# Modulation loads under the feed-forward products, moved to another queue and to half of the steps, and two copies moved between engines

## The chip, the cores and the metric

The kernel runs on one core of a Trainium2 chip. The metric is the device time of one execution in microseconds; a kernel's time is the median of several executions. The engines of the core work side by side: TensorE (PE, with its weight loads shown apart as PEld), VectorE (DVE), ScalarE (ACT), GpSimd (POOL) and SyncE (SP). SP here does nothing but start transfers between the main memory and the on-chip memory; GpSimd starts some too. An engine's instructions run in the order of its queue.

## What is computed

One layer of a hybrid encoder block on 512 tokens of width 2048, in 32-bit floats, and a final norm. The reference, cut to what matters here:

```python
c_act = jax.nn.silu(c)                       # c: one row of 2048
mod = c_act @ w_ada[l] + b_ada[l]            # 2048 x 12288: six rows of 2048
sh1, sc1, g1, sh2, sc2, g2 = split(mod, 6)
h = rms_norm(x, norm1_w[l]) * (1.0 + sc1) + sh1
qa, ka, va, qb, kb, vb, ga, gb = split(h @ w_in[l])
ya = global_gqa(...); yb = neighbourhood_attention(...)
merged = sigmoid(ga) * (ya @ w_oa[l]) + sigmoid(gb) * (yb @ w_ob[l])
x = x + g1 * (merged @ w_out[l])
h2 = rms_norm(x, norm2_w[l]) * (1.0 + sc2) + sh2
ff = (silu(h2 @ w_ffn_gate[l]) * (h2 @ w_ffn_up[l])) @ w_ffn_down[l]
x = x + g2 * ff
return rms_norm(x, final_w)
```

`g2` is needed only where `ff` is added, at the very end. It is one row times a 2048 x 2048 part of `w_ada`, which is 16 MB to be read.

## The kernel before

**Products.** Each float is split into a high part in the type that TensorE multiplies (fp32r) and a low part that holds the rest, and a product is three: high by high, high by low, low by high (`mm3`, lines 141 to 143). `split` (lines 132 to 134) makes the parts: the high one by a copy on ScalarE, the low one by a subtraction on VectorE. Weights come from main memory as raw tiles of 512 KB (`raw`, loaded by SP on line 148) and are split into `whl`. There are five buffers of each kind from the output projection on: four and three in one pool, one and two in a pool `wq` that takes every fifth raw tile (`buffer`, lines 106 to 111).

**The feed-forward products.** Gate and up projections are computed in groups of 512 columns, eleven for the gate and eleven for the up weights; the first gate group is done in another way, so 21 groups remain (`group7`, line 873, called on line 981). A group multiplies by a scheme with seven block products in place of eight. It has four steps of a quarter of the depth each. A step loads two raw tiles, forms sums of their blocks (`ta`, `tb`, lines 838 to 841), splits them, and runs 84 matmuls. At the end of a group the seven sums are taken out of their banks and combined (lines 892 to 899); the next group's products go to the same banks, so its third product waits for line 896.

**The modulation under them.** The row `g2` is formed in four pieces of 512 (`ada_gate`, line 312), called gates below. For each, eight raw tiles of `w_ada` (two parts of 128 x 512 each) are loaded by SP (line 273), and each part is multiplied by its column of `c_act` and added to `acc` by VectorE (line 288): 16 sums per gate. GpSimd clears `acc` first (line 281), and SP puts the bias row into it (line 282). Then TensorE adds up over the 128 partitions (line 320, `total`), VectorE copies one row (line 322) and SP stores it (line 323). This is a background job: a generator in the list `bg`, of which `pump` (line 166) runs one piece per call. `group7` calls `pump` at its second, third and fourth step (line 878), after the step's weights and before its matmuls, so a raw tile of `w_ada` is loaded and used in the same call. `total` is set down in the list `soon` with a count and runs some calls later; with one buffer for `acc`, the generator then waits out three calls before the next gate begins. A gate takes 11 calls.

**The order.** The order of each engine's queue is fixed before the run by the framework, by program order as a priority, by when it expects operands and buffers to be there. It may draw an instruction forward past earlier ones of its engine: a sum of line 288 often stands among the weights of an earlier step. The raw tiles of the first pool go to whichever buffer is free; the one in `wq` is fixed.

**The merge.** Lines 707 to 714 compute `merged` in pairs of feature tiles, `j` in steps of two, and split each into `mx[j // 2]` (named `m0h`, `m0l` to `m7h`, `m7l`). Each pair takes two units of `w_oa` and two of `w_ob`. The output projection (`w_out_pass`, line 750) starts right behind the last pair and begins with the first feature tiles.

The lines the change touches:

Of the kernel before, what the change touches and what calls it, by code (L numbers as in the profile page):

```python
# [19 lines left out]
P = 128  # L20
D = 2048
T = 512
NT = T // P
KT = D // P
# [63 lines left out]
def encoder_block(ctx: ExitStack, tc, xp, xT, c, w_ada, ada1_w, b_ada, norm1_w, w_in, q_norm_w, k_norm_w, tb,  # L88
                  w_oa, w_ob, w_out, norm2_w, w_gate, w_up, w_down, final_w, rope, wmask, out):
    nc = tc.nc  # L90
    V, S, G = nc.vector, nc.scalar, nc.gpsimd
# [21 lines left out]
    def raw_tile(name="raw"):  # L113
        return buffer("raw", [P, 1024], F32, wbufs["raw"], name)
# [7 lines left out]
    def bank(tag):  # L122
        return ps.tile([P, 512], F32, tag=tag, name=tag, bufs={"mm": 4, "S": 2, "T": 1, "Y": 1}[tag])
# [8 lines left out]
    def split(hi, lo, src, eng=V):  # L132
        S.activation(hi, src, AF.Copy)  # L133
        eng.tensor_sub(lo, src, hi)  # L134
# [5 lines left out]
    def mm3(o, lh, ll, rh, rl, start, stop, **kw):  # L140
        nc.tensor.matmul(o, lh, rh, start=start, stop=False, **kw)  # L141
        nc.tensor.matmul(o, lh, rl, start=False, stop=False, **kw)  # L142
        nc.tensor.matmul(o, ll, rh, start=False, stop=stop, **kw)  # L143

    def unit(w, k0, nk, c0, ncol):
        raw = raw_tile()
        r3 = raw[:, :nk * ncol].rearrange("p (k n) -> p k n", k=nk)
        nc.sync.dma_start(r3, w[k0 * P:(k0 + nk) * P, c0:c0 + ncol].rearrange("(k p) n -> p k n", p=P))
        return raw[:, :nk * ncol], r3
# [8 lines left out]
    bg = []  # L158
# [3 lines left out]
    soon = []  # L162
# [3 lines left out]
    def pump():  # L166
        due = [f for n, f in soon if n <= 0]
        soon[:] = [(n - 1, f) for n, f in soon if n > 0]
        for f in due:
            f()  # L170
        if later:
            later.pop(0)()
        for _ in range(pace["steps"]):
            advance()

    def advance():
        if bg:
            try:
                next(bg[0])
            except StopIteration:  # L180
                bg.pop(0)
                advance()

    def form1(ws, c0, g, xs, banks, evac, eng=V):

        nk = 8 // g
        n = len(xs)
        for k0 in range(0, n, nk):
            m = min(nk, n - k0)
            for w, bs in zip(ws, banks):  # L190
                hi, lo = wsplit(w, k0, m, c0, g * P, eng)
                for kk in range(m):
                    xh, xl = xs[k0 + kk]
                    for j in range(g):
                        sl = slice(j * P, (j + 1) * P)
                        mm3(bs[j], hi[:, kk, sl], lo[:, kk, sl], xh, xl, k0 + kk == 0, k0 + kk == n - 1)
                pump()
        for wi, bs in enumerate(banks):
            for j in range(g):
                evac(wi, j, bs[j])  # L200
# [58 lines left out]
    t2 = const.tile([P, KT], F32, name="t2")  # L259

    accp = aside
    ada_room = {"bank": "Y", "bufs": 2}

    def ada_units(cols, w):

        nj = len(cols)
        nk = 1024 // (nj * w)
        for k0 in range(0, KT, nk):
            raw = raw_tile()
            r4 = raw.rearrange("p (k c n) -> p k c n", k=nk, c=nj)  # L270
            for j, col in enumerate(cols):
                src = w_ada[k0 * P:(k0 + nk) * P, col:col + w]
                nc.sync.dma_start(r4[:, :, j], src.rearrange("(k p) n -> p k n", p=P))
            yield [(k0 + e, raw[:, e * nj * w:(e + 1) * nj * w]) for e in range(nk)]

    def ada_acc(cols, w, bias):


        acc = accp.tile([P, 512], F32, tag="acc", name="acc", bufs=ada_room["bufs"])[:, :len(cols) * w]
        if bias:  # L280
            G.memset(acc, 0.0)
            nc.sync.dma_start(acc[0:1, :], b_ada[:, cols[0]:cols[0] + w])
        for parts in ada_units(cols, w):
            for k, part in parts:
                if k == 0 and not bias:
                    V.tensor_scalar(acc, part, cact[:, k:k + 1], None, op0=ALU.mult)
                else:
                    V.scalar_tensor_tensor(acc, part, cact[:, k:k + 1], acc, op0=ALU.mult, op1=ALU.add)  # L288
            yield None
        yield acc  # L290
# [21 lines left out]
    def ada_gate(col, q, dst):  # L312

        for acc in ada_acc((col + q * 512,), 512, True):
            if acc is None:
                yield

        def total():
            y = bank(ada_room["bank"])
            nc.tensor.matmul(y, ones, acc, start=True, stop=True)  # L320
            o = io.tile([P, 512], F32, tag="io", name="ada_o")
            V.tensor_copy(o[0:1, :], y[0:1, :])
            nc.sync.dma_start(dst[q], o[0:1, :])

        soon.append((1, total))
        if ada_room["bufs"] == 1:
            yield
            yield
            yield

    def rows(dst, src):
# [261 lines left out]
    bg.extend(ada_mod(3 * D, 4 * D, k, 2, (s2, b_sc2, n2, t2, b_sh2)) for k in range(0, KT, 2))  # L593
    g1_d, g2_d = ([dram.tile([1, 512], F32, name=f"g{n}d{q}") for q in range(4)] for n in (1, 2))
    bg.extend(ada_gate(2 * D, q, g1_d) for q in range(4))
    pace["steps"] = 2
    gates(sg_b, GB, 0, 8)
# [78 lines left out]
    def half(t, n=2):  # L676
        return t.rearrange("p (a q n) -> p a q n", q=2, n=256) if n == 2 else t.rearrange("p (q n) -> p q n", q=2)
# [15 lines left out]
    mT = [tuple(Tokens(half(t)[:, :, k % 2]) for t in mx[k // 2]) for k in range(KT)]  # L693

    def gated(src, dst):
        def evac(w, j, b):
            g = io.tile([P, T], F32, tag="io", name="g")
            nc.sync.dma_start(g, src[j])
            if any(src[j] is t for t in sg_a[:12]):
                S.activation(g, g, AF.Sigmoid)  # L700
            o = p_y.tile([P, T], F32, tag="o", name="o", bufs=4)
            V.tensor_mul(o, g, b)
            dst.append(o)
        return evac

    turn = itertools.cycle(("mm", "mm", "S"))
    for j in range(0, KT, 2):
        ma, mb = [], []
        for w, ys, sg, to in ((w_oa, yT[:8], sg_a, ma), (w_ob, yT[8:], sg_b, mb)):
            tag = next(turn)  # L710
            form1([w], j * P, 2, ys, [[bank(tag), bank(tag)]], gated(sg[j:], to))
        for e in range(2):
            V.tensor_add(ma[e], ma[e], mb[e])
            split(*(t.t for t in mT[j + e]), ma[e].rearrange("p (t n) -> p t n", t=2))
    p_y.release()
    aside.release()
    wq = tc.alloc_tile_pool(name="wq", bufs=1, side="right", reuse_waits="tile")
# [86 lines left out]
    norm((2, 3))  # L804
    gpool.release()
    accp = tc.alloc_tile_pool(name="accp", bufs=1, side="left", reuse_waits="tile")
    ada_room.update(bank="T", bufs=1)

# [62 lines left out]
    def group7(wsrc, xs, order, dst):  # L873

        bk = {r: bank(BANK[r]) for r in ORDER}
        for n, s in enumerate(order):
            w = wsrc(s)
            if n:
                pump()
            for r in ORDER:  # L880
                (wh, wl), (xh, xl) = w[r], xs[s][r]
                for q in range(2):
                    for c in range(2):
                        o = bk[r][:, c * 256:(c + 1) * 256]
                        cs = slice(c * P, (c + 1) * P)
                        first, last = n == 0 and q == 0 and c == 0, n == len(order) - 1 and q == 1
                        mm3(o, wh[:, q, cs], wl[:, q, cs], xh[:, q], xl[:, q], first, last, skip_group_check=True)
        p = {r: b.rearrange("p (c n) -> p c n", c=2) for r, b in bk.items()}
        (d11, d12), (d21, d22) = dst
        with tc.high_priority():  # L890
            p1 = io.tile([P, 512], F32, tag="io", name="p1").rearrange("p (c n) -> p c n", c=2)
            S.activation(p1, p[1], AF.Copy)
            V.tensor_add(d11, p[2], p1)
            V.tensor_add(d21, p[6], p1)
            V.tensor_add(d12, p[5], d21)
            V.tensor_add(d12, p[3], d12)  # L896
            V.tensor_add(d21, p[7], d21)
            V.tensor_add(d22, p[5], d21)  # L898
            V.tensor_sub(d21, d21, p[4])
# [9 lines left out]
    parts = [(s, a) for s in (2, 3, 0, 1) for a in range(2)]  # L909
# [54 lines left out]
    for n in range(FU):  # L964
        cs = []
        for w in (w_gate, w_up):
# [8 lines left out]
            def wsrc(s):  # L975
                d = wforms(w, 4 * s, n * 512)
                if s == 1 and n == FU - 1 and w is w_up:
                    first_pairs()
                return d
# [6 lines left out]
            V.tensor_mul(cs[1][:, sl], cs[1][:, sl], cs[0][:, sl])  # L986
        (nc.sync if n < FU - 1 else nc.gpsimd).dma_start(ff_d[n], cs[1])

    wbufs["at"] = 0
    for p in (c_p, f_x[1], f_x[0], ca, f_x[3], f_x[2], accp, p_m):  # L990
        p.release()
# [122 lines left out]
    ahead = {}  # L1114
# [70 lines left out]
    for cc in range(2, 4):  # L1185
        wt = p_s.tile([P, 4096 + 64], F32R, tag=f"a{3 - cc}", name=f"w{cc}")
        hi, lo = (wt[:, 48 + e * 2048:48 + (e + 1) * 2048] for e in range(2))
        for k in range(0, 4, 2):
            raw, _ = unit(w_down, f0 + k, 2, cc * 512, 512)
# [55 lines left out]
```

## Time and profile before

| what | value |
|---|---|
| time, median of 3 runs | 2639.69 us (2639.11 to 2649.6) |
| profiled execution | 2644.09 us, its span 2642.3 us |
| granted TensorE clock, mean | 0.992 |
| TensorE busy | 2569.5 us, 97% |
| VectorE busy | 1913.7 us, 72% |
| ScalarE busy | 1029.5 us, 39% |
| GpSimd busy | 95.1 us, 4% |
| groups of seven products end | 21 times, from about 1351 to 2150 us |
| last modulation sum | 1864.6 us |

How to read the profile: a row of a group of instructions gives line, engine, operation, the tile written and those read, how often, and durations in ns (least, median, most). A row of waits gives the engine and line that waited, what ended the wait, and total, number and longest in us. A row of the order of time gives start and duration in us, and in brackets how long the engine was idle before and what ended that. A row of a stretch gives its bounds and length, the busy time of PE, PEld, DVE, ACT and POOL with the number of instructions, the granted clock, and the DMA engines' share and rate. A busy TensorE isn't necessarily at its quickest, since its matmuls overlap.

### The profile page before, as it was taken

The numbers are of one execution on the slowest core, as the hardware profiler recorded it, in microseconds if no ns is written. First come the engines' busy times: TensorE is split into PE (matmuls) and PEld (weight loads), VectorE is DVE, ScalarE is ACT, GpSimd is POOL, SyncE is SP. The second block draws the span as 40 slices with busy tenths as digits, with TensorE's granted clock in tenths as the row PEclk, the third lists the DMA queues.
The fourth block names the chain that finished last, engine by engine and source line by source line (L and its number), as shares of the span: only waits on it lengthen the run. The fifth ranks groups of instructions, "written<-read, shape, count | busy, mean of one in ns | idle before, by whom it ended". The sixth has DMA issues, their size and how long they took to land. (4 is left out here: it accounts for less than half of the span.)

```text
span 2642.3 us, 40965 instructions
## 1 busy us (share of the span) xinstructions
PE 2569.5 (97%) x16569; PEld 2320.3 (88%) x16569; DVE 1913.7 (72%) x2708; ACT 1029.5 (39%) x1406; POOL 95.1 (4%) x134
## 2 busy tenths in 40 slices
PE   6999999999999999999999999999999999999998
PEld 5788878888788888788999999999999997999997
DVE  7985787766746544336798888888888885678767
ACT  5223544223333332226644433444444454334233
POOL 0100000001010000011000000000000000000000
PEclk8999999999999999999999999999999999999999
DMA  8864245974735844546454444545434456447463
GB/s 315 303 242 146 64 152 171 302 231 148 227 106 167 264 156 144 182 130 218 120 182 136 139 152 136 161 127 160 129 124 124 130 171 223 163 144 246 149 254 109
DMA packets 251949, 458.77 MB, mean 174 GB/s; under 512 B 16112, under 2 KB 102496, under 8 KB 243312
## 3 DMA queue, kind: packets, MB, share of 16 engines
q1 hardware_dynamic: 238208, 381.64, 45.3%
q0 software_dynamic: 12064, 71.31, 7.6%
q10 hardware_dynamic: 1488, 3.20, 0.3%
q8 instruction: 130, 2.13, 0.3%
q14 instruction: 59, 0.48, 0.1%
HBM read 412.03 MB, written 44.06 MB: 173 GB/s over the span
## 5 line engine op out<-in xcount | busy, mean ns | idle before, releaser
L133 ACT ACTIVATE whl<-raw 128x1024 fp32r<-128x1024 f32 (+1 forms) x483 | 463.6, 962 | 862.7 <-PE mm L143 274.4
L134 DVE TENSOR_TENSOR whl<-raw,whl 128x1024 fp32r<-128x1024 f32 (+1 forms) x483 | 533.2, 1113 | 309.9 <-ACT whl L133 301.5
L288 DVE SCALAR_TENSOR_TENSOR acc<-raw,cact,acc 128x512 f32<-128x512 f32 x248 | 187.3, 755 | 43.6 <-DMA raw<-in_w_ada 37.5
L133 ACT ACTIVATE whl<-tb 128x1024 fp32r<-128x1024 f32 x104 | 110.5, 1063 | 175.0 <-PE S L143 137.8
L133 ACT ACTIVATE whl<-ta 128x1024 fp32r<-128x1024 f32 x104 | 110.3, 1061 | 173.2 <-PE mm L143 123.8
L134 DVE TENSOR_TENSOR whl<-ta,whl 128x1024 fp32r<-128x1024 f32 x104 | 127.2, 1223 | 46.0 <-ACT whl L133 45.5
L134 DVE TENSOR_TENSOR whl<-tb,whl 128x1024 fp32r<-128x1024 f32 x104 | 127.0, 1221 | 15.6 <-ACT whl L133 14.5
L141 PE MATMUL mm<-x3h,whl 128*128 128x256 f32 x336 | 94.8, 282 | 13.6 <-DVE c L896 13.6
L838 DVE TENSOR_TENSOR ta<-raw 128x512 f32<-128x512 f32 x104 | 71.8, 690 | 49.1 <-DMA raw<-in_w_down 35.1
L141 PE MATMUL mm<-whl,a 128*128 128x256 f32 (+1 forms) x304 | 97.9, 322 | 3.5 <-ACT acc L1105 3.5
L839 DVE TENSOR_TENSOR ta<-raw,ta 128x512 f32<-128x512 f32 x104 | 71.7, 690 | 39.9 <-DMA raw<-in_w_down 22.2
L142 PE MATMUL mm<-whl,a 128*128 128x256 f32 (+1 forms) x304 | 97.8, 322 | 0.2 <-DVE whl L134 0.2
L143 PE MATMUL mm<-whl,a 128*128 128x256 f32 (+1 forms) x304 | 97.7, 321 | 0.0
L141 PE MATMUL mm<-x56h,whl 128*128 128x256 f32 x336 | 94.4, 281 | 1.3 <-DVE c L898 0.7
L142 PE MATMUL mm<-x3l,whl 128*128 128x256 f32 x336 | 94.2, 280 | 0.0
L143 PE MATMUL mm<-x3h,whl 128*128 128x256 f32 x336 | 94.1, 280 | 0.0
L142 PE MATMUL mm<-x56l,whl 128*128 128x256 f32 x336 | 93.8, 279 | 0.0
L143 PE MATMUL mm<-x56h,whl 128*128 128x256 f32 x336 | 93.7, 279 | 0.0
L143 PE MATMUL S<-x56h,whl 128*128 128x256 f32 x336 | 93.6, 279 | 0.0
L142 PE MATMUL S<-x56l,whl 128*128 128x256 f32 x336 | 93.6, 279 | 0.0
L141 PE MATMUL S<-x56h,whl 128*128 128x256 f32 x336 | 93.6, 279 | 0.0
L142 PE MATMUL mm<-whl,s 128*128 128x256 f32 x320 | 90.6, 283 | 2.2 <-DVE whl L134 2.2
(1479 smaller groups left out, 8508.7 us busy)
## 6 DMA issues: line engine op xcount, KB each, us to landing
raw<-in_w_in SPq DMA_DIRECT2D x133, 512.0 KB
raw<-in_w_gate SPq DMA_DIRECT2D x92, 512.0 KB
raw<-in_w_up SPq DMA_DIRECT2D x88, 512.0 KB
raw<-in_w_down SPq DMA_DIRECT2D x88, 512.0 KB
raw<-in_w_ada SPq DMA_DIRECT2D x128, 256.0 KB
raw<-in_w_ada SPq DMA_DIRECT2D x64, 512.0 KB
raw<-in_ada_w POOLq DMA_DIRECT2D x29, 1024.0 KB, 6.7
raw<-in_w_out SPq DMA_DIRECT2D x48, 512.0 KB
```

What stands on the lines that cost most here:

```text
L133: S.activation(hi, src, AF.Copy)
L134: eng.tensor_sub(lo, src, hi)
L141: nc.tensor.matmul(o, lh, rh, start=start, stop=False, **kw)
L142: nc.tensor.matmul(o, lh, rl, start=False, stop=False, **kw)
L143: nc.tensor.matmul(o, ll, rh, start=False, stop=stop, **kw)
L288: V.scalar_tensor_tensor(acc, part, cact[:, k:k + 1], acc, op0=ALU.mult, op1=ALU.add)
L838: V.tensor_sub(t1, b12, b11)
L839: V.tensor_sub(t2_, b22, t1)
```

## The change

The generator of the loads can run one load ahead: it keeps a list `ready`, and a call first issues the next load and then hands out the one before. Under the feed-forward products (`ahead=1`) the first call of a gate only loads, and the sums of a tile come one call after its load. The loads there are issued on GpSimd's queue. `group7` calls `pump` at its third and fourth step only. `total` is set down with count 0 in place of 1 and the generator waits out one call in place of three, so a gate takes 10 calls. After the groups a loop runs whatever is left. Before the feed-forward products (`ahead` 0, SP's queue, two buffers for `acc`) the job is as it was.

Apart from this, the high parts of the last two merged tiles (`j` = 14) are copied by VectorE instead of ScalarE.

```diff
-    ada_room = {"bank": "Y", "bufs": 2}
+    ada_room = {"bank": "Y", "bufs": 2, "ahead": 0, "queue": nc.sync}
...
-        for k0 in range(0, KT, nk):
+        def load(k0):
             raw = raw_tile()
             r4 = raw.rearrange("p (k c n) -> p k c n", k=nk, c=nj)
             for j, col in enumerate(cols):
                 src = w_ada[k0 * P:(k0 + nk) * P, col:col + w]
-                nc.sync.dma_start(r4[:, :, j], src.rearrange("(k p) n -> p k n", p=P))
-            yield [(k0 + e, raw[:, e * nj * w:(e + 1) * nj * w]) for e in range(nk)]
+                ada_room["queue"].dma_start(r4[:, :, j], src.rearrange("(k p) n -> p k n", p=P))
+            return [(k0 + e, raw[:, e * nj * w:(e + 1) * nj * w]) for e in range(nk)]
+
+        ready = []
+        for k0 in range(0, KT, nk):
+            ready.append(load(k0))
+            yield ready.pop(0) if len(ready) > ada_room["ahead"] else None
+        yield from ready
...
         for parts in ada_units(cols, w):
+            if parts is None:
+                yield None
+                continue
...
-        soon.append((1, total))
+        soon.append((ada_room["bufs"] - 1, total))
         if ada_room["bufs"] == 1:
-            yield
-            yield
             yield
...
-            split(*(t.t for t in mT[j + e]), ma[e].rearrange("p (t n) -> p t n", t=2))
+            (mh, ml), o3 = (t.t for t in mT[j + e]), ma[e].rearrange("p (t n) -> p t n", t=2)
+            if j + 2 < KT:
+                split(mh, ml, o3)
+            else:
+                V.tensor_copy(mh, o3)
+                V.tensor_sub(ml, o3, mh)
...
-    ada_room.update(bank="T", bufs=1)
+    ada_room.update(bank="T", bufs=1, ahead=1, queue=nc.gpsimd)
...
-            if n:
+            if n > 1:
                 pump()
...
+    while bg or soon:
+        pump()
     wbufs["at"] = 0
```

## The prediction

> **What bounds the kernel now.** I read the page's head first, then busy time by stretches, then who waited for whom under the feed-forward products, and last the order of time around two stalls.
>
> ```profile
> span 2642.3 us, 40965 instructions
> PE 2569.5 (97%) x16569; PEld 2320.3 (88%) x16569; DVE 1913.7 (72%) x2708; ACT 1029.5 (39%) x1406; POOL 95.1 (4%) x134
> ...
> L892 ACT ACTIVATE p<-mm x21: 597/599/600, 1350.8 to 2149.7; 128x512 f32<-128x512 f32 x21
> ...
> 1350.80:1921.20 570.40, 555.49 (x4714) 550.82 (x4714) 489.02 (x626) 233.23 (x246) 1.58 (x3) 1.00 0.46 144
> 1921.20:2149.70 228.50, 228.50 (x2018) 228.50 (x2017) 191.83 (x237) 102.30 (x108) 0.57 (x1) 1.00 0.42 129
> 1575.00:1605.00 30.00, 30.00 (x257) 30.00 (x256) 23.91 (x31) 11.94 (x13) 0.00 (x0) 1.00 0.40 120
> 1915.00:1945.00 30.00, 30.00 (x267) 30.00 (x266) 27.37 (x34) 12.46 (x14) 0.00 (x0) 1.00 0.43 137
> ```
>
> TensorE is busy for 97% of the span, so only its gaps and its pace can be won. L892 runs once at the end of each of the 21 groups of seven products, so the first stretch is 14 groups and the second is six (the columns are the stretch, then PE, weight loads, DVE, ACT, POOL, and the granted clock). The modulation steps lie under the first stretch and are over before the second. The six clean groups take 228.5 / 6 = 38.08 us each with no PE gap; the 14 with modulation take 570.4 / 14 = 40.74 us. What modulation costs there is 570.4 - 14 x 38.08 = 37.3 us.
>
> That loss has two parts. PE idle is 570.40 - 555.49 = 14.9 us. The other 22.4 us is inside the busy time: of the last two rows both are full and both at clock 1.00, yet one holds 257 matmuls and the other 267. TensorE has two paces here, 116.7 and 112.4 ns per matmul, which is 4.3 ns x 336 = 1.45 us per group. I can't say from the trace what sets the pace; the clean stretch begins in the quick one and, having no gap, stays in it.
>
> The idle part comes from VectorE running late at the seam between two groups:
>
> ```profile
> DVE acc L288 <- DMA raw<-in_w_ada: 19.9, 12, 2.9
> PE mm L141 <- DVE c L896: 13.6, 8, 4.9
> DVE ta L839 <- DMA raw<-in_w_up: 10.3, 8, 3.1
> DVE ta L838 <- DMA raw<-in_w_gate: 6.5, 4, 2.7
> DVE ta L838 <- DMA raw<-in_w_up: 6.1, 6, 1.6
> DVE ta L839 <- DMA raw<-in_w_gate: 5.8, 4, 2.3
> PE mm L141 <- ACT c L971: 3.0, 1, 3.0
> DVE acc L288 <- issue: 2.2, 1, 2.2
> ...
> 1399.25 0.75 DVE L288 SCALAR_TENSOR_TENSOR acc<-raw,cact,acc 128x512 f32<-128x512 f32 x1 [1.63 <-DMA raw<-in_w_ada]
> ...
> 1404.29 0.36 PE L141 MATMUL mm<-x3h,whl 128*128 128x256 f32 x1 [1.65 <-DVE c L896]
> ...
> 1520.00:1527.00 7.00, 2.57 (x23) 2.37 (x21) 5.01 (x8) 1.64 (x2) 0.00 (x0) 1.00 0.39 135
> 1527.00:1531.00 4.00, 3.51 (x17) 3.54 (x18) 4.00 (x7) 0.58 (x1) 0.00 (x0) 0.57 0.06 5
> ```
>
> The first eight rows are the waits from 1310 to 1922 us (total, times, longest). VectorE's queue is in order. At 1399.25 a modulation sum stood in front of the evacuation of the old group's banks and waited 1.63 us for its own load; the third product of the next group then waited 1.65 us for L896, the add that frees its bank. Eight such seams make 13.6 us of the 14.9. Modulation loads account for 19.9 us of VectorE's DMA waits, weight loads for 28.7 (the four L838 and L839 rows). The worst seam, 4.9 us, was followed by 4 us at clock 0.57 that hold 17 matmuls where the quick pace has 35: 2.0 us more, part of the 22.4.
>
> **The change part by part.** *The steps themselves.* Four gates x 8 loads x 2 sums stay: 64 sums under the groups before and after. They move from steps 2, 3 and 4 of each group to steps 3 and 4. A gate needs 10 calls of the background generator (eight loads, one that drains the last load, one that sets the total) where it needed 11; four gates need 40, and the total of the last one comes in the 41st. At two calls per group that is 20 groups and a bit out of 21, so modulation now lies under all of them and the six clean groups are lost as such. The loop behind the groups finds nothing left.
>
> ```profile
> L288 DVE SCALAR_TENSOR_TENSOR acc<-raw,cact,acc x248: 732/752/1494, 356.1 to 1864.6; 128x512 f32<-128x512 f32 x124
> L320 PE MATMUL T<-acc,ones x8: 590/591/594, 1459.2 to 1909.7; 128*128 128x512 f32 x8
> SPq L148 <- DMA raw<-in_w_ada: 35.0, 11, 4.8
> L273 SPq DMA_DIRECT2D raw<-in_w_ada x192: 367/384/1256, 352.1 to 1857.1; - x192
> L954 POOL DMA_DIRECT2D ffr<-ffd x12: 528/528/568, 2143.4 to 2437.4; - x12
> ffr<-ffd POOLq DMA_DIRECT2D x12, 512.0 KB, 5.4
> L281 POOL MEMSET acc<- x8: 526/527/530, 625.2 to 1760.7; 128x512 f32 x8
> ```
>
> VectorE's load: a group with three steps carries 6 x 0.75 = 4.5 us of sums, with two 3.0 us; the clean groups show 191.83 / 6 = 32.0 us of VectorE work in 38.08, so 35 us fits and VectorE does not become the bound. The four totals (two matmuls of 0.59 us each) stay: 4.7 us before and after, also part of the 22.4.
>
> *The queue.* 32 issues of 0.38 us leave SP and become 32 of 0.53 us on POOL, 17 us in all on an engine with 95.1 us of work. Nothing else issues there until the end of the loop except four memsets of 0.53 us; the load of a gate's first part now stands behind its memset, which waits for the total of the gate before, and the step's lead covers that. Without that cover it would cost the 5.4 us that a 512 KB load of POOL's takes to land, three times. In front of SP's weight loads the waits for modulation data go away as a matter of order (35.0 us of that queue's time, 11 times), though a weight load whose buffer still holds a modulation part waits as before. The bias row stays on SP and now has a step more to land; the 2.2 us wait on "issue" goes. It is in the idle count.
>
> The Trainium skill ("DMA: Bandwidth & Descriptors", section "Issuing engines are not separate DMA queues") says that starting transfers from several engines saves no more than the time it takes to start them. By that rule the new queue would free 32 x 0.38 = 12 us of SP and add nothing to the sum. The row of 35.0 us shows more than issue time at stake, since the loads behind stood in line; it reaches TensorE only through VectorE's waits, which are counted next.
>
> *Idle time after.* No row shows the new order, so I bound it. Lowest: 0, as in the clean groups. Highest: the present 14.9 / 14 = 1.06 us per group in all 21, 22.3. If the modulation waits vanish and the weight waits stay, 28.7 / 48.6 of it is left, 8.8 us; two loads in place of three per group take that to about 5.9, if it goes with the number of loads. I take 6: a gain of 8.9. The stall that made the clock drop is then gone too: 2.0. What is late next at a seam is a weight load of L838 or L839.
>
> *The pace.* Of the 22.4 us, 4.7 are totals and 2.0 the slow clock; 15.7 are slow pace, about 11 groups of 1.45. After: between 0 (always quick) and 21 x 1.45 = 30.5. With disturbances in all groups I take half of them slow, 15.2: a gain of 0.5.
>
> *The copies of the last merged tiles.* These are one edit with one place:
>
> ```profile
> 1066.26 1.06 ACT L133 ACTIVATE whl<-raw 128x1024 fp32r<-128x1024 f32 x1 [2.93 <-PE S L143]
> 1083.85 1.24 ACT L133 ACTIVATE m7h<-o 128x512 fp32r<-128x512 f32 x2 [16.53 <-DVE o L713]
> 1084.99 4.83 ACT L133 ACTIVATE whl<-raw 128x1024 fp32r<-128x1024 f32 x5
> ...
> 1087.97 1.22 PE L141 MATMUL mm<-whl,m0h 128*128 128x512 f32 x2 [5.49 <-ACT whl L133]
> ...
> 1079.80 0.37 SPq L148 DMA_DIRECT2D raw<-in_w_out  x1
> ...
> 1087.00:1094.00 7.00, 5.61 (x13) 3.98 (x14) 4.83 (x5) 2.81 (x3) 0.00 (x0) 0.51 0.62 174
> 1094.00:1100.00 6.00, 6.00 (x28) 4.98 (x27) 1.23 (x1) 1.06 (x1) 0.00 (x0) 1.00 1.02 382
> ...
> L286 DVE TENSOR_SCALAR acc<-raw,cact x8: 477/486/489, 355.6 to 588.1; 128x512 f32<-128x512 f32 x8
> L365 DVE COPY call<-mm x2: 692/692/693, 16.4 to 19.3; 128x512 f32<-128x512 f32 x2
> ```
>
> ScalarE stood 16.53 us in front of the two m7h copies with the five weight copies of the output projection behind them. PE resumed at 1087.97, when the third of those had ended (1084.99 + 3 x 0.97). Without the m7h copies the third can go when its data is there: issued at 1079.80, some 5.4 us to land, plus 1.06: 1086.3, so 1.7 us earlier. The low part then must not be late on VectorE, which gets two copies more, 0.49 to 0.69 each (from the nearest one-input rows; nearer 0.49, whose source is SBUF too). Behind the gap came 7 us at clock 0.51 with 13 matmuls, where the next row's rate would take 2.8. A gap of 3.0 us (L971 above) brought no such drop and one of 4.9 did; about 4 us lies between, so I count half of the roughly 3 us of slow clock. Sum: a gain of 3. Bounds: 9 (gap and drop gone) and a loss of 1 (VectorE's two copies in front of the low part).
>
> **Sum.** 8.9 + 2.0 + 0.5 + 3.0 = 14.4 us less than the profiled execution's 2644.1 (1.8 us lie around its span) gives 2629.7. The median of the runs, 2639.7, is 4.4 below that execution, so I forecast 2625 us.
>
> **The rivals.** *Full gain:* no idle, quick pace throughout, the seam at 1087 closed: 14.9 + 2.0 + 15.7 + 9 = 41.6, so 2598. For it: six clean groups in a row do exist. Against it: the four totals disturb TensorE anyway, and the weight waits are not touched.
>
> *No change:* the order of VectorE's queue is fixed ahead, and a sum may be drawn forward to where its load was expected to land. Then each of the same 32 loads is waited for as now, at other places: idle 14.9, pace as now, and at 1087 nothing: 2639 to 2641. For it: the number of loads and sums is the same. Against it: the seam's wait at 1399 stands behind a step that no longer exists. The rule of the Trainium skill quoted above, taken for the queue alone, would end here too.
>
> *Slower:* the ring of load buffers. There are five; a group took 11 and takes 10, but a part loaded in step 4 is summed in step 3 of the next group, with six weight loads between. Whenever its buffer isn't given back early, the next weight load waits for it, and with SP's queue in order all loads behind wait too. One buffer of the five is a pool of its own, used by every fifth load; counting the loads, the parts of step 4 fall on it throughout the fourth gate, and the weight load that wants it next is that of the very step whose sum frees it. The price is that all 21 groups cost what the 14 do: six more x 2.66 = 16 us, so 2656; with the fourth gate's four groups at one more 5 us load each, 20 more. It decides where the loss per group stays above 37.3 / 21 = 1.8 us. For it: VectorE waits 28.7 us for weights already. Against it: two loads per group in place of three.
>
> **How the numbers follow.** Forecast, 2612 to 2634 by its own bounds: 0.43. Full gain, under 2612: 0.12. No change: 0.24. Slower: 0.21. A difference of 0.5%, 13 us, is about what a measurement of this kernel can tell from none. Of the forecast about three quarters lies below 2626.5; so faster 0.45, same 0.34, slower 0.21. The range 2600 to 2658 reaches from nearly full gain to just past the slower case without the fourth gate's extra.
>
> **What would show it.** Right: the waits of L288 for in_w_ada fall from 19.9 us to under 5; PE's wait for L896 falls to 6 or less over 21 groups; modulation loads stand in POOL's queue up to about 2110 us; PE resumes near 1086 at the output projection. Wrong: groups after 1921 at over 40 us, L838 and L839 waiting longer for weights than 28.7 us, SP waiting for L288, or PE resuming after 1088 because the low part on VectorE came late. If the idle time falls and the groups still take 39.6 us, it was the pace.

## The result and the profile after

The changed kernel takes 2632.57 us (median; 2624.41 to 2639.13), the kernel before, run beside it, 2648.36 us (2634.5 to 2656.67). The ratio is 0.995, with a 95% interval of 0.9934 to 0.9965: 0.5% faster. The forecast was 2625 us with a range of 2600 to 2658. The profiled execution of the changed kernel took 2638.57 us. In that kernel the lines have moved: the sum L288 is L298, the weight sums L838 and L839 are L851 and L852, the first evacuation L892 is L905, and the add L896 that frees the third product's bank is L909.

The head of its page, and then two views: busy time by stretches (the 14 groups and the six groups of before, then 30 us from each of two parts, both without a gap) and the waits from 1310 to 2150 us (VectorE's, TensorE's and, last, the one row of SP's queue).

```profile
span 2636.8 us, 40994 instructions
PE 2575.5 (98%) x16569; PEld 2328.0 (88%) x16569; DVE 1912.8 (73%) x2710; ACT 1030.0 (39%) x1404; POOL 119.0 (5%) x166
```

```profile
1349.30:1921.20 571.90, 571.22 (x4835) 569.73 (x4835) 492.92 (x627) 239.96 (x252) 17.74 (x25) 1.00 0.44 139
1921.20:2141.00 219.80, 218.12 (x1898) 216.47 (x1896) 188.51 (x238) 96.21 (x101) 6.17 (x9) 1.00 0.47 149
1575.00:1605.00 30.00, 30.00 (x257) 30.00 (x257) 25.25 (x33) 12.28 (x14) 0.72 (x1) 1.00 0.33 111
1985.00:2015.00 30.00, 30.00 (x268) 30.00 (x267) 28.67 (x37) 12.77 (x15) 1.46 (x2) 1.00 0.47 158
```

```profile
DVE ta L851 <- DMA raw<-in_w_up: 18.1, 13, 3.1
DVE ta L852 <- DMA raw<-in_w_up: 11.5, 8, 3.4
DVE ta L851 <- DMA raw<-in_w_gate: 9.1, 7, 1.9
DVE ta L852 <- DMA raw<-in_w_gate: 8.5, 8, 1.8
DVE acc L298 <- DMA raw<-in_w_ada: 4.5, 6, 1.3
...
PE mm L141 <- ACT c L984: 2.1, 1, 2.1
PE mm L141 <- DVE c L909: 1.9, 3, 1.0
...
SPq L148 <- DMA raw<-in_w_ada: 13.2, 7, 2.4
```

TensorE now idles 0.68 + 1.68 = 2.4 us in the 20 groups, where it idled 14.9. Its wait for the add that frees the bank has gone from 13.6 us to 1.9, and VectorE's wait for modulation loads from 19.9 to 4.5. The weight waits of L851 and L852 have risen, from 29.3 us before (10.9 + 6.5 + 6.1 + 5.8 over the same 1310 to 2150) to 47.2, and cost TensorE little: the three waits for L909 that are left, 1.9 us, all stand behind such a weight wait. At one of them TensorE waited 0.50 us, and VectorE before it:

```profile
1555.73 0.69 DVE L851 TENSOR_TENSOR ta<-raw 128x512 f32<-128x512 f32 x1 [2.09 <-DMA raw<-in_w_up]
```

The 20 groups from the first to the last L905 take 2141.0 - 1349.3 = 791.7 us, 7.2 less than before (2149.7 - 1350.8 = 798.9). Idle gave 12.5 and the slow clock behind the worst seam, which no longer exists, 2.0. But the pace took back 7.3: against 20 x 38.08 = 761.6 us the groups lose 30.1 us, of which 2.4 is idle and 4.7 the totals, so 23.0 is slow pace, where it was 15.7. The two last rows of the stretches show the paces again, 257 and 268 matmuls in 30 us at clock 1.00. This profile happens to run slow until 1936 us. From first to last profile the gain is 5.5 us; between the medians it is 15.8. The experiments on the pace below bear on the difference.

At the output projection nothing was won. The order of time there, in the changed kernel:

```profile
1080.03 1.37 DVE L710 TENSOR_TENSOR o<-g,mm 128x512 f32<-128x512 f32 x2 [9.51 <-PE mm L143]
1080.29 0.39 PE L143 MATMUL mm<-y15h,whl 128*128 128x512 f32 x1
1080.71 1.06 ACT L133 ACTIVATE whl<-raw 128x1024 fp32r<-128x1024 f32 x1 [15.21 <-PE mm L143]
1081.32 1.29 DVE L721 TENSOR_TENSOR o<-o 128x512 f32<-128x512 f32 x2
1082.52 0.76 DVE L726 CAST m7h<-o 128x512 fp32r<-128x512 f32 x2
1083.19 1.29 DVE L727 TENSOR_TENSOR m7l<-o,m7h 128x512 fp32r<-128x512 f32 x2
1084.39 5.89 DVE L134 TENSOR_TENSOR whl<-raw,whl 128x1024 fp32r<-128x1024 f32 x5
1084.56 3.90 ACT L133 ACTIVATE whl<-raw 128x1024 fp32r<-128x1024 f32 x4 [2.79 <-DVE m7l L727]
1086.62 1.22 PE L141 MATMUL mm<-whl,m0h 128*128 128x512 f32 x2 [5.95 <-ACT whl L133]
```

ScalarE no longer copies m7h, yet it waits nearly as long as before (16.53 us): 15.21 us, for TensorE's last products, and then 2.79 us for m7l. TensorE's gap, start to start, is 1086.62 - 1080.29 = 6.33 us, where it was 1087.97 - 1082.10 = 5.87.

### The profile page after: what moved, and what is told of

It is laid out like the page before. It is cut to its first block, busy times and chain, and to the rows that moved or that the text cites. A ratio compares the mean times of both kernels' runs of the same rounds, so it can differ in the third digit from the quotient of the medians.

```text
span 2636.8 us, 40994 instructions
## 1 busy us (share of the span) xinstructions
PE 2575.5 (98%) x16569; PEld 2328.0 (88%) x16569; DVE 1912.8 (73%) x2710; ACT 1030.0 (39%) x1404; POOL 119.0 (5%) x166
## 4 chain that ended last, share of the span: by engine, by line
PE 86%; DVE 6%; DMA 5%; issue 1%; ACT 1%; SPq 0%; DVEq 0%; ACTq 0%; POOLq 0%
PE mm L141 18%; PE mm L142 18%; PE mm L143 18%; PE S L141 6%; PE S L143 6%; PE S L142 6%; PE Y L141 3%; PE Y L142 3%; PE Y L143 3%; DVE whl L134 2%; DMA raw<-in_w_in 2%; DMA raw<-in_w_up 1%; DVE acc L298 1%; PE T L143 1%; PE T L142 1%
## 5 line engine op out<-in xcount | busy, mean ns | idle before, releaser
L134 DVE TENSOR_TENSOR whl<-raw,whl 128x1024 fp32r<-128x1024 f32 (+1 forms) x483 | 532.7, 1114 | 312.1 <-ACT whl L133 302.2
L298 DVE SCALAR_TENSOR_TENSOR acc<-raw,cact,acc 128x512 f32<-128x512 f32 x248 | 187.2, 755 | 27.8 <-DMA raw<-in_w_ada 22.4
L134 DVE TENSOR_TENSOR whl<-ta,whl 128x1024 fp32r<-128x1024 f32 x104 | 127.4, 1225 | 39.8 <-ACT whl L133 39.8
L134 DVE TENSOR_TENSOR whl<-tb,whl 128x1024 fp32r<-128x1024 f32 x104 | 127.0, 1221 | 15.3 <-ACT whl L133 14.7
L851 DVE TENSOR_TENSOR ta<-raw 128x512 f32<-128x512 f32 x104 | 71.9, 691 | 65.5 <-DMA raw<-in_w_down 36.9
L852 DVE TENSOR_TENSOR ta<-raw,ta 128x512 f32<-128x512 f32 x104 | 71.7, 690 | 42.9 <-DMA raw<-in_w_down 22.2
```

The source lines that it names most:

```text
L851: V.tensor_sub(t1, b12, b11)
L852: V.tensor_sub(t2_, b22, t1)
```

## The experiments

The theory behind the first four kernels: the gain comes from the two calls in the back half of a group, since a modulation sum then no longer stands at the seam between two groups; the step's lead, GpSimd's queue and the VectorE copies add nothing. The rivals: the lead gives the load time to land and is what counts; SP's queue was what held the weights; the copies are worth some 3 us.

### One part of the change at a time

`copy_only` is the kernel before with the VectorE copies alone:

```diff
-            split(*(t.t for t in mT[j + e]), ma[e].rearrange("p (t n) -> p t n", t=2))
+            (mh, ml), o3 = (t.t for t in mT[j + e]), ma[e].rearrange("p (t n) -> p t n", t=2)
+            if j + 2 < KT:
+                split(mh, ml, o3)
+            else:
+                V.tensor_copy(mh, o3)
+                V.tensor_sub(ml, o3, mh)
```

> The kernel before with the copies of the last merged tiles on VectorE and nothing else. Theory A (the wait only changes its name): ScalarE's second weight copy of the output projection writes over the tiles that the m7l subtractions read, so it waits for them, and TensorE's gap there stays at 5.5 to 6.5 us: within 2 us of the kernel before. Theory B (the prediction's term): TensorE resumes about 2 us earlier, 3 us in the time, 0.1%.

Measured: ratio 1.0007 (0.9987 to 1.0027), gap 6.33 us. The copies alone are worth nothing.

`half_only` is the kernel before with two calls per group, both loads and sums in one call on SP's queue, and ScalarE's copies:

```diff
-            if n:
+            if n > 1:
                 pump()
...
-        soon.append((1, total))
+        soon.append((ada_room["bufs"] - 1, total))
         if ada_room["bufs"] == 1:
-            yield
-            yield
             yield
```

> The kernel before with the modulation calls in the back half of each group only (and the shorter pause behind a gate, 9 calls): no lead, loads on SP's queue, copies on ScalarE. Theory A (fewer loads per group is what counts): the idle time at the seams falls from 14.9 us to 6 or less although VectorE still waits for modulation loads; 8 to 12 us faster than before. Theory B (the lead and the queue are what counts): VectorE's waits for modulation loads stay near 20 us, the idle time at 10 us or more; at most 4 us faster.

Measured: ratio 0.9936 (0.9915 to 0.9958), 2629.2 us: all of the gain. Its waits from 1310 to 2160 us:

```profile
DVE ta L847 <- DMA raw<-in_w_up: 11.7, 8, 2.1
DVE ta L847 <- DMA raw<-in_w_gate: 9.9, 6, 3.1
DVE ta L846 <- DMA raw<-in_w_gate: 6.0, 4, 2.1
DVE acc L298 <- DMA raw<-in_w_ada: 4.0, 2, 2.1
DVE ta L846 <- DMA raw<-in_w_up: 3.5, 4, 1.6
...
PE mm L141 <- ACT c L979: 2.7, 1, 2.7
```

TensorE has no wait left for the add that frees the bank (here L904), though VectorE waits 31.1 us for weights (11.7 + 9.9 + 6.0 + 3.5). What counts is where a wait stands. In `half_only` VectorE waits for no load between the first of the adds that take the seven sums out of their banks (L901) and the add that frees the bank. In the kernel before, nine such waits stand there (L893 to L896): three of modulation sums, 5.4 us in all, and six of weight sums, 7.6 us. At five of the eight seams where TensorE waits, the last wait was a weight sum's, and at five a modulation sum had also waited in front of the first add (1.1 to 2.9 us). This is the weight sum at the seam where TensorE waited 3.08 us:

```profile
1688.41 0.69 DVE L838 TENSOR_TENSOR ta<-raw 128x512 f32<-128x512 f32 x1 [2.65 <-DMA raw<-in_w_gate]
```

`half_lead_sp` adds the lead, but leaves the loads in SP's queue; `lead_pool_three` has the lead and GpSimd's queue, but three calls per group as before:

```diff
+    ada_room.update(bank="T", bufs=1, ahead=1)                   # half_lead_sp, with n > 1
...
+    ada_room.update(bank="T", bufs=1, ahead=1, queue=nc.gpsimd)  # lead_pool_three, with n > 0
```

> Back half of each group and a lead of one call, but the loads on SP's queue; copies on ScalarE. If the lead is what removes the waits for modulation loads, they are under 4 us here too and the time is that of the changed kernel, 13 us below before. If GpSimd's queue is needed, SP still waits about 35 us for modulation data and VectorE about 15 us or more for modulation loads, and the gain is under 8 us.

> Lead of one call and GpSimd's queue, but three calls per group, so that modulation ends near 1870 us as before; copies on ScalarE. If fewer loads per group is what counts, the seams stall as before (idle 10 us or more in the 14 groups) and the gain is under 5 us. If lead and queue are what counts, idle falls to 5 us or less and the time is that of the changed kernel or lower, since six groups stay free of modulation.

Measured: 0.9944 (0.9928 to 0.996) with the lead on SP's queue, 1.0028 (1.001 to 1.0045) with lead and GpSimd's queue and three calls. Neither lead nor queue is worth anything, and without the back half they lose a little. Two waits of the last kernel from 1310 to 2160 us:

```profile
DVE acc L298 <- DMA raw<-in_w_ada: 17.8, 12, 3.6
...
PE mm L141 <- DVE c L904: 16.5, 8, 3.8
```

Even with the loads a call ahead in program order, and in GpSimd's queue, VectorE waits for them 12 times, and TensorE waits at eight seams.

### Fewer loads, or their place

`front_half` has two calls per group as `half_only`, at the second and third step:

```diff
-            if n > 1:
+            if 0 < n < 3:
                 pump()
```

> Two calls per group as in the kernel with calls at the third and fourth step only (2629.2 us, ratio 0.9936, excess of the gaps over 20 groups 3.1 us), but at the second and third step. Theory A (what counts is that a group has two loads in place of three): the excess of the gaps is 6 us or less and the ratio 0.992 to 0.996. Theory B (what counts is the place, the back half): the step behind a seam has its load again, sums are drawn into the seam and wait there as before, excess 10 to 20 us, ratio 0.997 to 1.001.

Measured: ratio 0.9993 (0.998 to 1.0007), 2645.97 us. TensorE idles 11.4 us in the 20 groups, where it idled 14.9 in the kernel before and 0.1 in `half_only`. Its waits from 1310 to 2160 us:

```profile
DVE acc L298 <- DMA raw<-in_w_ada: 26.1, 15, 2.8
...
PE mm L141 <- DVE c L904: 10.3, 9, 2.9
```

Same number of loads, of calls and of sums as in `half_only`, and the gain is gone: it is the place. At all nine seams where TensorE waits for L904, a modulation sum waits for its load in front of the first add (1.2 to 2.8 us), and between the first add and the freeing add loads are waited for eleven times, eight of them weights. The largest of TensorE's waits, and the weight wait in front of it:

```profile
1798.03 0.69 DVE L846 TENSOR_TENSOR ta<-raw 128x512 f32<-128x512 f32 x1 [1.70 <-DMA raw<-in_w_up]
...
1802.40 0.55 PE L141 MATMUL mm<-x3h,whl 128*128 128x256 f32 x1 [2.87 <-DVE c L904]
```

So a sum at the seam that waits for its load, of either kind, holds the bank. With the calls in the back half no load is waited for between the two adds in `half_only`, and two weights (4.2 us) in the changed kernel. That the modulation loads are what makes the weights late at the seam fits `no_mod` below, where they are gone and weights are hardly waited for; that it is so at each seam is not shown.

### The pace

`no_mod` does not compute the row `g2`, so that nothing disturbs TensorE under the groups; its output lacks the feed-forward part:

```diff
-    bg.extend(ada_gate(5 * D, q, g2_d) for q in range(4))
+    for q in range(4):
+        o = io.tile([P, 512], F32, tag="io", name="ada_o")
+        G.memset(o[0:1, :], 0.0)
+        nc.sync.dma_start(g2_d[q], o[0:1, :])
```

> The modulation row g2 is not computed: its four pieces are stored as zeros, so 32 loads, 64 sums and four totals are gone from under the feed-forward products, and the output lacks the feed-forward part. Nothing disturbs TensorE there. Theory A (a disturbance sets the slow pace, and without one the quick pace stays): all 20 groups at 38.1 us, 762 us in all, 26 us under the two-call kernel's 787.9: 2600 to 2606 us, ratio 0.982 to 0.985. Theory B (the pace is a toss at the start of the stretch and then stays): the 20 groups take either 762 or 791 us, and the times of the executions fall into two clusters about 30 us apart, near 2603 and 2633 us. Theory C (the slow pace comes from VectorE and ScalarE load or weight loads, not from disturbances): paces mixed with no disturbance between, about 778 us.

Measured: median 2603.82 us, but the single times were 2595.69, 2601.7, 2602.53, 2605.1, and 2629.19, 2632.09. They fall into two clusters with nothing between. Another execution of the same program gave 2599.58 us:

> The kernel without the g2 row once more (it stores zeros for the row and its output lacks the feed-forward part). In the first profile all 20 groups took 39.57 us. Theory A (a toss that then stays): with a time near 2603 us all groups take 38.1 us, with one near 2630 us 39.57 us; no mixture. Theory B: the groups take 39.57 us again whatever the time.

The stretch from 1360 to 2040 us and the row of L892, first of the execution of 2632.09 us, then of that of 2599.58 us:

```profile
1360.00:2040.00 680.00, 680.00 (x5776) 680.00 (x5775) 557.18 (x690) 287.03 (x302) 0.00 (x0) 1.00 0.40 121
...
L892 ACT ACTIVATE p<-mm x21: 598/598/602, 1351.1 to 2142.5; 128x512 f32<-128x512 f32 x21
```

```profile
1360.00:2040.00 680.00, 680.00 (x6003) 680.00 (x6002) 575.71 (x713) 297.20 (x312) 0.00 (x0) 1.00 0.41 126
...
L892 ACT ACTIVATE p<-mm x21: 598/598/599, 1349.4 to 2110.9; 128x512 f32<-128x512 f32 x21
```

Both are full of matmuls from end to end, at clock 1.00, with no gap. One does 5776 in 680 us, 117.7 ns each, the other 6003, 113.3 ns each. Its 20 groups take 791.4 us in the one and 761.5 in the other, 39.57 or 38.08 us each, to within 0.1 us. The theory that a disturbance makes the pace slow has fallen: undisturbed, the slow pace stays too. In the traces of the kernel before, the changed kernel, `half_only` and `front_half` the pace of these groups changes only where the even distance of the matmul starts is broken, by a wait, sometimes of only 0.1 us, or by a total, and not in between; at many breaks it stays as it was. So a disturbance lets the pace be drawn again. (VectorE's weight waits, too, are down to a single one of 0.2 us in both: the modulation loads are what makes weights late.)

`after_again` is the changed kernel, profiled a second time:

> The changed kernel once more, for a second profile of the same program. Theory A (the pace is a toss at each disturbance): the quick and the slow stretches lie at other places than in the first profile (slow from 1319 to 1936, then quick), with the same waits. Theory B (the program sets the pace): the same stretches.

The time was 2632.63 us. The waits were much the same (3.0 us for L909, 5.2 for modulation loads), the paces were not:

```profile
1420.00:1530.00 110.00, 110.00 (x936) 110.00 (x936) 93.08 (x117) 45.22 (x48) 2.18 (x3) 1.00 0.41 130
1580.00:1730.00 150.00, 150.00 (x1326) 150.00 (x1326) 131.80 (x168) 65.61 (x69) 4.22 (x6) 1.00 0.45 141
1760.00:1930.00 170.00, 170.00 (x1445) 170.00 (x1445) 147.87 (x186) 71.20 (x75) 5.07 (x7) 1.00 0.46 144
```

From 1580 to 1730 us it runs 113.1 ns per matmul, where the first profile ran the slow pace all the way to 1936. Counted by the distance of starts, 48% of the matmuls of the 20 groups were slow here and 75% in the first profile; in the kernel before it was 45%. The same instructions in the same order meet another pace: the program alone doesn't set it.

### Three queues in turn at the output projection

The copies won nothing, so something else held TensorE there. The pool `wq` is set up right behind the release of the merge's tiles, on the same side of the on-chip memory. ScalarE's two waits above, for the last products with y15 and for m7l, are what weight copies would wait for whose buffers lie over the last y tiles and the `o` tiles, which are in use up to the end. `half_y` is `half_only` with the tiles in another order, so that these buffers lie over y0 to y7, which are done earlier. `half_y_copy` adds the VectorE copies to it (the edit of `copy_only`):

```diff
-    yT = [pair(p_y, f"y{k}", T, 1) for k in range(KT)]
+    o_first = [p_y.tile([P, T], F32, tag="o", name="o_first", bufs=4) for _ in range(4)]
+    yT = [pair(p_y, f"y{k}", T, 1) for k in [*range(8, KT), *range(8)]]
+    yT = yT[8:] + yT[:8]
```

> Two calls per group without the lead and without GpSimd's queue, copies on ScalarE, and the order of the merge's tiles turned: the four o tiles and y8 to y15 come first, y0 to y7 last, so the two weight buffers and the raw buffer of wq lie over y0 to y7, whose last products run before those of y8 to y15. Theory A (the gap of 5.9 to 6.3 us at the output projection comes from those buffers: the first weight copies wait for what lay there): PE's gap at the first product with m0h falls under 2 us and the half clock behind it goes, 5 to 9 us against the same kernel without this (2629.2 us, ratio 0.9936): 2620 to 2624 us, ratio 0.990 to 0.992. Theory B (the ScalarE copies m7h, which stand in front of the weight copies, hold them, as my prediction had it): the gap stays at 4 us or more, 2627 to 2630 us.

> As the kernel with the turned order of the merge's tiles, and the high parts of the last two merged tiles copied by VectorE. Theory A (the buffers alone): the gap and the time are those of the kernel without the VectorE copies, within 0.1% of it. Theory B (both hold the weight copies): the gap is at 4 us or more without the VectorE copies and under 2.5 us with them, 3 to 6 us between the two. Theory C: the copies on VectorE come late for the low part, and the time is 1 to 3 us above.

Measured: `half_y` 0.9933 (0.9914 to 0.9952), gap 5.87 us as in the kernel before; `half_y_copy` 0.993 (0.9909 to 0.995), and the gap has only moved (none of its three theories had it so; the third came nearest, with a far smaller price). In `half_y` the row of waits reads as in the kernel before, ScalarE behind m7h:

```profile
ACT m7h L133 <- DVE o L723: 16.5, 1, 16.5
...
PE mm L141 <- ACT whl L133: 5.5, 1, 5.5
```

In `half_y_copy`, the order of time:

```profile
1077.08 1.06 ACT L133 ACTIVATE whl<-raw 128x1024 fp32r<-128x1024 f32 x1 [3.06 <-DMA raw<-in_w_out]
1078.39 1.06 ACT L133 ACTIVATE whl<-raw 128x1024 fp32r<-128x1024 f32 x1 [0.26 <-PE mm L143]
1083.15 1.37 DVE L712 TENSOR_TENSOR o<-g,mm 128x512 f32<-128x512 f32 x2 [9.51 <-PE mm L143]
1083.63 0.61 PE L141 MATMUL mm<-whl,m0h 128*128 128x512 f32 x2
1087.52 4.62 DVE L134 TENSOR_TENSOR whl<-raw,whl 128x1024 fp32r<-128x1024 f32 x4
1091.06 0.80 PE L142 MATMUL mm<-whl,m0h 128*128 128x512 f32 x1 [6.81 <-DVE whl L134]
```

ScalarE's weight copies are now done before the merge ends, and TensorE starts at once with the high part. Then it stands 7.2 us for the low part, which VectorE makes (L134): VectorE had waited 9.51 us in front of the last merged tiles and did their eight instructions first. `half_y_copy_g` lets GpSimd make the low parts of the first two weight tiles:

```diff
-            hi, lo = wsplit(w, r0 + k0, m, c0, 512, eng)
+            hi, lo = wsplit(w, r0 + k0, m, c0, 512, eng if k0 >= early else G)   # early = 4 in the first pass, else 0
```

> As the kernel with two calls per group, the turned order of the merge's tiles and the VectorE copies (its gap of 7.2 us at the output projection ended with VectorE's low parts of the first weights, line 134, which stand behind six instructions of the last merged tiles), but the low parts of the first two weight tiles of the output projection are made by GpSimd. Theory A (three queues in turn hold PE there: ScalarE's order, then the buffers, then VectorE's order; with all three gone nothing is left): the gap falls from 7.2 to under 1.5 us and the clock behind it stays at 1.00, 6 to 10 us less than the same kernel without this (2631.9 us): 2622 to 2626 us, ratio 0.989 to 0.991. Theory B (something else is late next, the data or the banks): the gap stays at 3 us or more and the time within 3 us.

Measured: 2623.24 us, ratio 0.9909 (0.9886 to 0.9932), faster than the kernel before and the changed one. The step from the last product with y15 to the first with m0h is 0.23 us, the usual distance, so no gap is left. `half_y_g` takes the VectorE copies out of that again:

> As the fastest kernel so far (two calls per group, turned order of the merge's tiles, VectorE copies, low parts of the first two output-projection weights on GpSimd: 2623.2 us, gap 0.2 us), but with the last merged tiles' high parts copied by ScalarE as in the kernel before. Theory A (all three queues have to be freed, and the VectorE copies are one of the three): ScalarE's weight copies stand behind the m7h copies again, the gap at the output projection is 5 to 6 us and the time 4 to 9 us more, 2627 to 2632 us. Theory B (the buffers and GpSimd's low parts do it alone, the VectorE copies are worth nothing anywhere): gap under 1.5 us, 2621 to 2626 us.

Measured: 2633.61 us, ratio 0.9945 (0.9924 to 0.9966), gap 5.87 us. The stretch behind the seam, first of `half_y_copy_g`, then of `half_y_g`:

```profile
1083.00:1090.00 7.00, 7.00 (x32) 5.79 (x31) 4.70 (x5) 1.06 (x1) 0.00 (x0) 1.00 1.02 375
```

```profile
1084.00:1091.00 7.00, 1.22 (x2) 0.50 (x2) 5.70 (x7) 5.97 (x7) 3.94 (x2) 0.73 0.46 159
1091.00:1098.00 7.00, 5.25 (x13) 4.16 (x14) 3.92 (x2) 0.00 (x0) 1.70 (x1) 0.54 0.74 245
```

Without the copies 30 + 19 = 49 matmuls are missing in 14 us, at 7.00 / 32 us each 10.7 us; between the medians lie 10.4. Not all of that is the copies': in `half_y_g` TensorE waits a second time, 2.61 us, for the low part on GpSimd (2.85 us each there, 1.2 on VectorE), where `half_y` waits 0.4. From `half_y`, which has neither, to `half_y_copy_g` the medians fall by 7.7 us, and that is what copies and GpSimd's low parts are worth together. Without the copies GpSimd's low parts gain nothing, and the copies alone, or with the buffers alone, gain nothing. Whether copies and GpSimd's low parts would do without the new order of the tiles was not tried.

## Why the prediction was right, and where it was not

*The sum.* 14.4 us were forecast and 15.8 lie between the medians. But it came out by a swap: the seams gave more, the output projection nothing. That the sum came so close is in part luck.

*The steps themselves* held: VectorE, at 681 us of 792, did not become the bound, and four gates of ten calls end in the last groups. The last load is issued at 2046.7 us, earlier than the 2110 I named, since the last calls of a gate load nothing.

*Idle time after* was mis-sized: 2.4 us instead of 6, a gain of 12.5 instead of 8.9 (in the second profile 3.5 us are left). The failed step is "if the modulation waits vanish and the weight waits stay, 28.7 / 48.6 of it is left". I shared TensorE's idle time out over VectorE's waits by their sum, but only a wait at the seam counts: `half_only` has 31.1 us of weight waits, none of them between the first add and the add that frees the bank, and no TensorE wait behind them. My reading of the "Eight such seams" was wrong too, since at five of them the last wait was a weight sum's. That a weight load is what is late next at a seam was right: TensorE's last 1.9 us stand behind weights. That the *slow clock* behind the worst seam goes, 2.0, was right in the first profile; in the second a wait of 2.6 us is followed by 3.3 us at clock 0.50.

*The queue* was right in the sum (nothing of its own). The Trainium skill ("DMA: Bandwidth & Descriptors", section "Issuing engines are not separate DMA queues") would have it so, and the runs agree: 0.9944 on SP's queue and 0.995 on GpSimd's (the second has the VectorE copies too, which alone are worth nothing). The price of an issue was off, 0.73 us and not 0.53, as this row of the changed kernel shows. That cost nothing visible, since GpSimd waited 730 us in front of these issues anyway:

```profile
L274 POOL DMA_DIRECT2D raw<-in_w_ada x32 | 23.3, 727 | 730.4 <-DVE whl L134 432.6 <-DMA raw<-in_w_gate 133.5 <-DMA raw<-in_w_up 66.1
```

*The pace* I left at no gain to speak of (0.5), for the right reason: I could not say what sets it. But I took disturbances for what makes it slow, and that was wrong: it can change at a disturbance, either way, and stays until the next. In the profiles shown it took back 7.3 us; the second profile, with 48% slow, says that this was the draw of one execution. Whether the change moves the share of slow pace on average was not measured. It also spoiled the base: I set the forecast against a median of three, 2639.69, and with more executions the kernel before stood at 2648.36, 8.7 us higher. That is more than the forecast's error against the changed kernel, 2632.57 - 2625 = 7.6.

*The copies* failed as a term: 3 us forecast, 0 measured (ratio 1.0007). TensorE did resume at 1086.6, as I said it would, but because this execution reached the seam 1.8 us earlier; the gap itself was 6.33 us. The failed step is "without the m7h copies the third can go when its data is there": I took the first releaser that the profile named for the only one. Behind ScalarE's order stood the buffers of the merge's tiles, and behind these VectorE's low parts. My lower bound named VectorE's chain only as a small loss. The limit of "about 4 us" between gaps without and with a slow clock behind them doesn't hold either, as the last section shows.

*The rivals.* "No change" holds for the parts alone: with three calls (`lead_pool_three`) or two in front (`front_half`) VectorE goes on waiting at the seams. Its ground, that a sum is drawn forward to where its load was expected, is what `front_half` showed, where a modulation sum waits in front of the first add; the calls in the back half escape it. "Slower" did not come: weight waits did rise, with the lead (44.7 us in `half_lead_sp`, 47.2 in the changed kernel, 31.1 without it in `half_only`), and cost little, since only 4.2 us of the 47.2 stand between the two adds. "Full gain" would have needed all three queues at the output projection and the quick pace by luck.

## What to carry to other kernels

Don't share an engine's idle time out over the waits of the engine that feeds it by their length; look which waits stand right in front of the instruction that it waits for, whatever they wait for, and keep that place free of loads. When a wait has gone and the gap has not, ask what the next instruction in each queue would wait for (the queue's order, the buffer, the other half of the operand) and clear them together: here two of the three gained nothing. Where one program's executions can lie 30 us apart through TensorE's pace alone, compare medians of many, and read a pair of profiles by its stalls.

## What was not expected of the hardware

TensorE has two steady paces at a granted clock of 1.00 in the same stretch of the same program: 113.3 and 117.7 ns per 256-column matmul, 3.9% apart, 30 us over 20 groups. Either lasts 760 to 790 us when nothing disturbs it. The Trainium skill ("TensorE: Matmul & The Clock Gate", section "Part 1: The HAM clock gate") gives one distance of starts for a full clock, from which I estimate 256 / 2.4 + 2.5 = 109 ns here; both measured paces lie above it, and of a second one it says nothing. What draws the pace stays open: in both executions TensorE waits for nothing, the clock is 1.00 and the instructions are the same, and nothing was found that steers it.

The gap of 5.9 us in `half_y_g`, with a second wait of 2.6 us behind it, was followed by 7 us at a mean clock of 0.54, and `half_y_copy_g`, which has none, ran on at 1.00. The same section of the Trainium skill has an idle window of about 3.4 us after which the clock is halved; these two kernels agree. In the profiles with a single gap of 5.9 to 6.3 us here, gap and slow clock together cost 8.4 to 9.7 us, an estimate from the matmuls that are missing in 24 us. Shorter waits are less regular. Those of 3.0 us for L971 and 3.1 us for L896 in the kernel before had no slow clock behind them, but the same wait of 3.0 us (L979) in `half_lead_sp` had 3.4 us at 0.50, and so had one of only 2.3 us for L904 in `front_half`. So the length of a short wait alone does not tell here whether the clock is halved behind it.
